# Moving four low-part subtractions at the end of attention from VectorE to GpSimd in a two-layer decoder trunk

## The chip, the cores and the metric

The kernel runs on one core of a Trainium2 chip. Its time is the device time of one execution in microseconds (us); the median of three runs of the kernel before is 1260.38 us (1257.83 to 1261.02). The engines are named as in the profile: PE is TensorE (PEld its weight loads), DVE is VectorE, ACT is ScalarE, POOL is GpSimd and SP is SyncE, which issues most DMAs.

## The reference

A trunk of two layers over 512 tokens of 1024 features, in float32. Layer 0 mixes by a causal Conformer convolution, layer 1 by differential attention with 8 heads; each is followed by a SwiGLU feed-forward network (2816 hidden) and a gate that adds a projection of a second input `p`:

```
for i in range(DEPTH):                       # DEPTH = 2
    ...                                      # i = 0: h += conformer_conv(rms_norm(h))
    lambda_init = 0.8 - 0.6 * math.exp(-0.3 * i)
    u = rms_norm(h, attn_norm_g[j])
    h = h + diff_attention(u, ...)           # i = 1
    u = rms_norm(h, ffn_norm_g[i])
    h = h + swiglu(u, ffn_w_gate[i], ffn_w_up[i], ffn_w_down[i])
    gate = jax.nn.sigmoid(rms_norm(h, ple_norm_g[i]) @ ple_w_gate[i])
    h = h + gate * (p[i] @ ple_w_proj[i])

# in diff_attention, per block of 128 queries:
    probs = jax.nn.softmax(logits, axis=-1)              # two sets of logits per head
    w = probs[:, :, 0] - lam * probs[:, :, 1]
    return jnp.einsum('bhqk,bhkd->bhqd', w, v)
```

The product `p[i] @ ple_w_proj[i]` takes 256 features of `p` to 1024. The change touches its operands in layer 1.

## The kernel before

All features lie on the 128 partitions and tokens on the free axis, so the trunk is a set of 128x512 tiles. **Precision.** Every matrix product is done as three products of rounded operands (`mm3`, lines 164 to 166): each operand is split into a high part, rounded to the type fp32r, and a low part, the rest. The high part is a cast on ScalarE; the low part is a subtraction, raw minus high. For weights this is `weight()`: a DMA from SP into a raw tile `wraw` (two buffers), the cast at line 157 into `whi`, the subtraction at line 159 into `wlo` (four buffers each). Its argument `eng` says which engine subtracts: VectorE unless told otherwise. GpSimd is told for three of the weights of the q/k projections (`GLO`). For `p`, `pfeatures` loads two 128x512 halves, casts them at line 278 and subtracts at line 279: on GpSimd in layer 0, on VectorE in layer 1. In layer 1 its raw halves use the `wraw` buffers too, so that the order there is half 0, half 1, projection weight 0, projection weight 1, and then the weights of attention's output product, each of them loaded when the subtraction two places before it is done.

**Attention.** q/k projections for pairs of heads (`unit`) and value projections (`values`) run for each block of 128 tokens; between their products, stages of the softmax of earlier heads are placed. `unit` leaves q and k with their norms: a power on GpSimd (line 229, the inverse root), then a scaling on GpSimd (line 925). `unit_end` transposes the block on PE (line 931), copies it from PSUM by ScalarE (lines 939 and 940), makes a second copy on GpSimd (944) and the low parts on VectorE (947 and 949). The stages of a head `hd` and a query block `qb` are: `stage_s`, scores on PE (976, 977), add bias and take the maximum on VectorE (979, reads PSUM), exponential on ScalarE (983), and on VectorE the weights of the difference (986 to 988); `stage_t`, transpose on PE (996), cast on ScalarE (998), low part on VectorE (999); `stage_a`, products with the values on PE (1012, 1013), gather (1019, 1020) and after the last block the head's norm (1024 to 1034, with a power at 229 and a scaling at 1034 on GpSimd); `stage_o`, transpose (1041) and split for the output product (178, 179).

**The end of attention.** After the last value projection the eight projections of `p` (`project`) run, with the remaining stages placed between by `step()`: their weights are two `weight()` tiles, one for four projections each. Then the output product begins.

**Order.** The code above is written in one sequence; a scheduler then sets each engine's order by its own estimate of durations. Each engine works through its list strictly in that order, so an instruction that waits holds all that is behind it on its engine. Changing the engine of an instruction can change the lists of all engines.

Of the kernel before, what the change touches and what calls it, by code (L numbers as in the profile page):

```python
# [15 lines left out]
ALU = mybir.AluOpType  # L16
# [76 lines left out]
def trunk(ctx, tc, xT, pT, wts, diag, dww, vec, rel, onehot, lamv, out):  # L93
    nc = tc.nc
    V, A, G, T = nc.vector, nc.scalar, nc.gpsimd, nc.tensor
# [7 lines left out]
    def sb(shape, tag, bufs, dt=F32):  # L103
        uid[0] += 1
        return pool.tile(shape, dt, tag=tag, name=f"{tag}_{uid[0]}", bufs=bufs)
# [10 lines left out]
    f = lambda ap: ap.bitcast(F32)  # L116
# [29 lines left out]
    def weight(n=1024, pieces=1, between=(), eng=V, after=None):  # L146
        i = wnext[0]
        wnext[0] += 1
        raw = sb([P, 1024], "wraw", 2)
        hi = sb([P, 1024], "whi", 4, F32R)  # L150
        lo = sb([P, 1024], "wlo", 4, F32R)
        for k in range(pieces):
            cut = slice(k * n // pieces, (k + 1) * n // pieces)
            loaded[0] = nc.sync.dma_start(raw[:, cut], wts[i, :, cut])
            if k < len(between):
                between[k]()
            A.copy(hi[:, cut], raw[:, cut])  # L157
            with tc.issue_after(after.ins) if after else nullcontext():
                eng.tensor_tensor(lo[:, cut], raw[:, cut], f(hi[:, cut]), ALU.subtract)  # L159
        return hi, lo  # L160
# [107 lines left out]
    def pfeatures(layer, parts):  # L268
        for k, (hi, lo) in enumerate(parts):
            if layer == 0:  # L270
                if k == 0:
                    two = sb([P, 2, S], "B7", 1)
                    nc.sync.dma_start(two.rearrange("p a s -> p (a s)"), pT[layer])
                raw = two[:, k]
            else:
                raw = sb([P, 1024], "wraw", 2)[:, :S]
                nc.sync.dma_start(raw, pT[layer, :, k * S : (k + 1) * S])
            A.copy(hi, raw)
            (G if layer == 0 else V).tensor_tensor(lo, raw, f(hi), ALU.subtract)
        return parts  # L280


# [2 lines left out]
    def project(ph, m, w, o, step=lambda: None):  # L285

        acc = mm()
        for k in range(2):
            last_product[0] = mm3(acc, wpart(w, 2 * (m % 4) + k), ph[k], k == 0, k == 1)
            step()  # L290
        last_copy[0] = A.copy(o, acc)
        return o
# [169 lines left out]
    for c in range(NC):  # L462
        wa, wg = pairs[c]
        if c == 0:
            pg = half(wg)
            norm.diagonal()
            pa = half(wa)
            rb = norm.rows()
            ph = pfeatures(0, [(sb([P, S], t, 2, F32R), sb([P, S], t, 2, F32R)) for t in ("wth", "wtl")])
# [590 lines left out]
    for what, at, pace in QKV:  # L1060
        ws = slab(GLO if what == "q" and at > 0 else 0, P * at[1] if what == "v" else S)
        for tb in range(4):
            if (what, at, tb) == ("v", (6, 2), 0):
                ph = pfeatures(1, [both(sb([P, 2, S], t, 1, F32R)) for t in ("B0", "B1")])
            between = take(3 * pace[tb])
            between += [None] * (6 - len(between))
            if waiting:
                between.append(partial(unit_end, *waiting))
                waiting = None
            if what == "v":  # L1070
                values(at, ws, tb, between)
            else:
                waiting = unit(at, ws, tb, between)
# [4 lines left out]
    def step():  # L1078
        if stages:
            n, s = stages.pop(0)  # L1080
            s()
        else:
            n = 99
        while done[0] < NH and (n - LA - 3) // 4 > done[0]:
            stage_o(done[0])
            done[0] += 1

    pp = []
    for m in range(NC):
        if m % 4 == 0:  # L1090
            w = weight()
        step()
        if m % 2 == 0:
            o2 = sb([P, 2, S], f"B{m // 2 + 2}", 1) if m < 4 else sb([P, 2, S], f"C{m // 2 + 1}", 2)
        pp.append(project(ph, m, w, o2[:, m % 2], step))
# [155 lines left out]
```

## Time and profile before

| | |
|---|---|
| median of 3 runs | 1260.38 us (1257.83 to 1261.02) |
| the profiled execution | 1259.05 us, of which the span from first to last instruction is 1257.3 us |
| busy in the span | PE 1239.1, DVE 904.6, ACT 615.5, POOL 264.1 us |
| granted TensorE clock, mean | 0.998 |

The times in the rows count from the start of the span. A timeline row has the start, the duration, the engine, the line, the operation, its output and inputs by the program's names with buffer numbers left out, the shape, and in brackets the idle time of the engine before it and what ended that. The sums of busy time per stretch tell which engine sets the pace there; a wait row says who ended it. Rows of one line and engine that follow each other are merged (x2).

### The profile page before, as it was taken

How to read it: one execution, taken by the hardware profiler on the slowest of the kernel's cores; microseconds unless marked ns; L12 is line 12 of the kernel's file. 1: busy time of each engine (PE TensorE's matmuls, PEld its weight loads, DVE VectorE, ACT ScalarE, POOL GpSimd, SP SyncE). 2: the span in 40 equal slices, each digit the busy share in tenths (PEclk: the TensorE clock that was granted, in tenths of full speed). 3: DMA queues.
4: the chain of work that ended last, by engine and by line, in shares of the span. 5: the costliest groups of instructions: out<-in, count | busy, mean ns of one | idle time of the engine just before them, and what ended most of it. 6: DMA issues, size and time to landing. Idle time of an engine off the chain costs nothing.

```text
span 1257.3 us, 18628 instructions
## 1 busy us (share of the span) xinstructions
PE 1239.1 (99%) x7152; PEld 1086.2 (86%) x7152; DVE 904.6 (72%) x1482; ACT 615.5 (49%) x1023; POOL 264.1 (21%) x231
## 2 busy tenths in 40 slices
PE   9999999999999999999999998999999999999998
PEld 7888778898999899988888987878898999899887
DVE  6998755965588558667678889746965598468665
ACT  6743454543355235446566768634542355235441
POOL 2853522000001000042616633122000000000030
PEclk9999999999999999999999999999999999999999
DMA  8666223464466444243322214223554467444241
GB/s 298 199 194 179 74 76 109 131 164 129 122 176 181 137 110 122 67 147 96 90 92 76 76 48 129 85 67 101 151 156 145 103 182 184 137 109 117 77 134 67
DMA packets 60597, 158.39 MB, mean 126 GB/s; under 512 B 6451, under 2 KB 11059, under 8 KB 60508
## 3 DMA queue, kind: packets, MB, share of 16 engines
q1 hardware_dynamic: 53776, 136.99, 34.3%
q0 software_dynamic: 4608, 16.78, 8.2%
q10 hardware_dynamic: 2124, 3.43, 0.9%
q8 instruction: 56, 0.92, 0.3%
q14 instruction: 33, 0.27, 0.1%
HBM read 151.91 MB, written 4.21 MB: 124 GB/s over the span
## 4 chain that ended last, share of the span: by engine, by line
PE 96%; DVE 2%; ACT 1%; DMA 0%; issue 0%; SPq 0%; ACTq 0%
PE mm L164 26%; PE mm L165 25%; PE mm L166 25%; PE tp L166 2%; PE tp L165 2%; PE tp L164 2%; PE sc L370 2%; PE sc L165 1%; PE sc L166 1%; PE sc L164 1%; PE mm L1012 1%; PE sc L976 1%; PE sc L977 1%; PE tp L996 1%; PE mm L370 1%; PE mm L326 1%
## 5 line engine op out<-in xcount | busy, mean ns | idle before, releaser
L165 PE MATMUL mm<-A,whi 128*128 128x512 f32 (+1 forms) x904 | 311.6, 346 | 0.3 <-DVE A L575 0.3
L164 PE MATMUL mm<-A,wlo 128*128 128x512 f32 (+1 forms) x904 | 307.2, 345 | 4.7 <-DVE wlo L159 3.0
L166 PE MATMUL mm<-A,whi 128*128 128x512 f32 (+1 forms) x904 | 310.0, 343 | 0.0
L157 ACT CAST whi<-wraw 128x1024 fp32r<-128x1024 f32 (+2 forms) x150 | 151.3, 1015 | 225.4 <-PE mm L166 103.8
L159 DVE TENSOR_TENSOR wlo<-wraw,whi 128x1024 fp32r<-128x1024 f32 (+2 forms) x147 | 186.3, 1270 | 61.0 <-ACT whi L157 60.3
L164 PEld LDWEIGHTS mm<-A,wlo 128*128 128x128 f32 x904 | 171.4, 190 | 26.3 <-ACT A L178 2.5
L165 PEld LDWEIGHTS mm<-A,whi 128*128 128x128 f32 x904 | 171.5, 190 | 21.8 <-issue 1.2
L166 PEld LDWEIGHTS mm<-A,whi 128*128 128x128 f32 x904 | 171.6, 190 | 20.8 <-issue 1.4
L165 PE MATMUL mm<-B,whi 128*128 128x512 f32 x368 | 143.3, 390 | 0.0
L166 PE MATMUL mm<-B,whi 128*128 128x512 f32 x368 | 143.3, 390 | 0.0
L164 PE MATMUL mm<-B,wlo 128*128 128x512 f32 x368 | 141.1, 391 | 0.0
L681 POOL DMA_DIRECT2D C<-in_wts x32 | 28.1, 878 | 512.1 <-DVE h L792 178.2
L204 POOL TENSOR_TENSOR acc<-acc,wk 128x512 f32<-128x512 f32 x35 | 56.6, 1617 | 218.3 <-ACT wk L203 110.9
L166 PEld LDWEIGHTS mm<-B,whi 128*128 128x128 f32 x368 | 69.1, 188 | 15.0
L165 PEld LDWEIGHTS mm<-B,whi 128*128 128x128 f32 x368 | 69.1, 188 | 14.3
L164 PEld LDWEIGHTS mm<-B,wlo 128*128 128x128 f32 x368 | 69.1, 188 | 14.2
L166 PE MATMUL mm<-whi,A 128*128 128x512 f32 (+1 forms) x224 | 81.1, 363 | 0.0
L164 PE MATMUL mm<-whi,A 128*128 128x512 f32 (+1 forms) x224 | 80.9, 366 | 0.0
L165 PE MATMUL mm<-wlo,A 128*128 128x512 f32 (+1 forms) x224 | 80.8, 364 | 0.0
L792 DVE TENSOR_TENSOR h<-mm,h 128x512 f32<-128x512 f32 x48 | 33.0, 688 | 64.5 <-PE mm L166 64.5
L229 POOL TENSOR_TENSOR r<-v,mhalf 128x8 f32<-128x8 f32 (+1 forms) x31 | 46.2, 1490 | 120.9 <-DVE v L227 99.9
L674 DVE TENSOR_TENSOR wlo<-wraw,whi 128x1024 fp32r<-128x1024 f32 x32 | 39.2, 1225 | 33.5 <-ACT whi L673 33.4
(271 smaller groups left out, 2674.4 us busy)
## 6 DMA issues: line engine op xcount, KB each, us to landing
wraw<-in_wts SPq DMA_DIRECT2D x162, 512.0 KB, 3.6
C<-in_wts SPq DMA_DIRECT2D x32, 512.0 KB, 4.8
C<-in_wts POOLq DMA_DIRECT2D x32, 512.0 KB, 5.8
bias<-in_wts SPq DMA_DIRECT2D x32, 256.0 KB, 3.2
wraw<-in_wts SPq DMA_DIRECT2D x16, 384.0 KB, 3.1
D<-in_diag SPq DMA_DIRECT2D x22, 256.0 KB, 4.6
C<-in_diag SPq DMA_DIRECT2D x16, 256.0 KB, 4.7
h<-in_xT SPq DMA_DIRECT2D x8, 256.0 KB, 5.4
```

Source lines behind the costliest of these rows:

```text
L157: A.copy(hi[:, cut], raw[:, cut])
L159: eng.tensor_tensor(lo[:, cut], raw[:, cut], f(hi[:, cut]), ALU.subtract)
L164: T.matmul(acc, al, bh, start=first, stop=False)
L165: T.matmul(acc, ah, bl, start=False, stop=False)
L166: return T.matmul(acc, ah, bh, start=False, stop=last)
L204: self.last = self.eng.tensor_tensor(self.acc, self.acc, sq, ALU.add)
L229: last_pow[0] = G.tensor_tensor(r[:, :n], v[:, :n], mhalf[:, :n], ALU.pow)
L326: last_tap[0] = T.matmul(acc, dg[:, j % 4], ups[c][:, j : j + S], start=(j == 0), stop=(j == PE_TAPS[c] - 1))
L370: last_tap[0] = T.matmul(acc[:, g * P : (g + 1) * P], w, ups[c][:, g, LEAD - m : LEAD - m + P], start=(m == 0), stop=(m == LAGS - 1),)
L674: V.tensor_tensor(lo, raw, f(hi), ALU.subtract)
L681: nc.gpsimd.dma_start(q, wts[i + 2].rearrange("p (a s) -> p a s", a=2), accum_op=ALU.add)
L792: V.tensor_tensor(h[m], acc, h[m], ALU.add)
```

## The change

Two edits. In `pfeatures` the low parts of `p` are subtracted on GpSimd in layer 1 as in layer 0, and the two projection weights at the end of attention are asked for with `eng=G`, so that their low parts are subtracted on GpSimd. The casts, the loads and all products stay.

```diff
@@ pfeatures @@
             A.copy(hi, raw)
-            (G if layer == 0 else V).tensor_tensor(lo, raw, f(hi), ALU.subtract)
+            G.tensor_tensor(lo, raw, f(hi), ALU.subtract)
         return parts
@@ the loop over the eight projections of p @@
     for m in range(NC):
         if m % 4 == 0:
-            w = weight()
+            w = weight(eng=G)
         step()
```

The scheduler's lists change on four engines from there to the end of attention. GpSimd's list at this place, before (`big_7390` is the last q/k block of the last pair of heads, `D_1328` a head's output, the `r` are the powers):

```order
L944 CAST C_1297_7001<-C_1297_7001 64x2x128
L229 TENSOR_TENSOR r_1361_7300<-v_1360_7298,mhalf_71 128x4
L944 CAST C_1296_7000<-C_1296_7000 64x2x128
L944 CAST C_1297_7001<-C_1297_7001 64x2x128
L1034 TENSOR_TENSOR D_1328_7133<-D_1328_7133,r_1361_7300 128x512
L229 TENSOR_TENSOR r_1383_7398<-v_1382_7396,mhalf_71 128x8
L925 TENSOR_TENSOR big_7390<-big_7390,r_1383_7398 128x512
```

and now, where `B_1390` and `B_1391` are the two low halves of `p` and `wlo_7652` and `wlo_7869` those of the two projection weights:

```order
L944 CAST C_1297_7001<-C_1297_7001 64x2x128
L279 TENSOR_TENSOR B_1390_7413<-wraw_7415,B_1390_7413 128x512
L279 TENSOR_TENSOR B_1391_7414<-wraw_7419,B_1391_7414 128x512
L229 TENSOR_TENSOR r_1361_7300<-v_1360_7298,mhalf_71 128x4
L944 CAST C_1296_7000<-C_1296_7000 64x2x128
L944 CAST C_1297_7001<-C_1297_7001 64x2x128
L1034 TENSOR_TENSOR D_1328_7133<-D_1328_7133,r_1361_7300 128x512
L229 TENSOR_TENSOR r_1383_7398<-v_1382_7396,mhalf_71 128x8
L159 TENSOR_TENSOR wlo_7652<-wraw_7650,whi_7651 128x1024
L159 TENSOR_TENSOR wlo_7869<-wraw_7867,whi_7868 128x1024
L925 TENSOR_TENSOR big_7390<-big_7390,r_1383_7398 128x512
```

The halves stand ahead of the power for `D_1328`, and the weights between the power for the last q/k block and the scaling of that block.

On PE the transpose of that block (`tp_7475`) stood ahead of the last value products of the query block that is under way (`mm_7499`). Before:

```order
L1012 MATMUL mm_7499<-B_1260_6829,wth_7459 128x256
L931 MATMUL tp_7475<-ident_65,big_7390 128x128 x4
L976 MATMUL sc_7587<-C_1192_6466,C_1190_6464 128x512
L977 MATMUL sc_7587<-C_1194_6468,C_1190_6464 128x512
L996 MATMUL tp_7527<-ident_65,big_7347 128x128
L1013 MATMUL mm_7499<-B_1260_6829,wtl_7460 128x128
L1012 MATMUL mm_7499<-B_1269_6887,wth_7459 128x256
...
L976 MATMUL sc_7703<-C_1296_7000,C_1294_6998 128x128
L977 MATMUL sc_7703<-C_1298_7002,C_1294_6998 128x128
L1012 MATMUL mm_7656<-B_1260_6829,wth_7529 128x256
L164 MATMUL mm_7696<-B_1390_7413,wlo_7652 128x512
```

Now these products come first, a score product of the next head (`sc_7740`) is taken forward, and the transpose stands behind them; `mm_7656`, which starts the next head's values, stands ahead of the projection (`mm_7696`) as before, now behind three more pairs of score products:

```order
L1012 MATMUL mm_7499<-B_1281_6971,wth_7459 128x256
L1013 MATMUL mm_7499<-B_1281_6971,wtl_7460 128x128
L976 MATMUL sc_7740<-C_1296_7000,C_1294_6998 128x256
L977 MATMUL sc_7740<-C_1298_7002,C_1294_6998 128x256
L931 MATMUL tp_7475<-ident_65,big_7390 128x128 x4
L996 MATMUL tp_7527<-ident_65,big_7347 128x128
L976 MATMUL sc_7703<-C_1297_7001,C_1295_6999 128x128
L977 MATMUL sc_7703<-C_1299_7003,C_1295_6999 128x128
L976 MATMUL sc_7740<-C_1297_7001,C_1295_6999 128x256
L977 MATMUL sc_7740<-C_1299_7003,C_1295_6999 128x256
L1012 MATMUL mm_7656<-B_1260_6829,wth_7529 128x256
L164 MATMUL mm_7696<-B_1390_7413,wlo_7652 128x512
```

On ScalarE the four copies of that block (`C_1294` to `C_1297`) stood ahead of the cast of the output product's first weight (`whi_8050`), with the cast `wth_7529`, which `mm_7656` reads, behind them. Before:

```order
L898 ACTIVATE B_1281_6971<-mm_7623,rcol_5628 128x2x128
L939 ACTIVATE C_1294_6998<-tp_7475,lam_5564 64x2x128
L940 ACTIVATE C_1296_7000<-tp_7475,vec_63 64x2x128
L939 ACTIVATE C_1295_6999<-tp_7475,lam_5564 64x2x128
L940 ACTIVATE C_1297_7001<-tp_7475,vec_63 64x2x128
L983 ACTIVATE acc_7518,st_7343<-acc_7518,st_7343 128x384
L157 CAST whi_8050<-wraw_8049 128x1024
L998 CAST wth_7529<-tp_7527 128x128
```

Now the gather and the square of a head (`D_1395`, `wk_7564`) and the cast of `whi_8050` stand ahead of the copies:

```order
L1019 COPY D_1395_7431<-mm_7499 128x256
L1024 ACTIVATE wk_7564<-D_1395_7431 128x512
L157 CAST whi_8050<-wraw_8049 128x1024
L939 ACTIVATE C_1294_6998<-tp_7475,lam_5564 64x2x128
L940 ACTIVATE C_1296_7000<-tp_7475,vec_63 64x2x128
L939 ACTIVATE C_1295_6999<-tp_7475,lam_5564 64x2x128
L940 ACTIVATE C_1297_7001<-tp_7475,vec_63 64x2x128
L998 CAST wth_7529<-tp_7527 128x128
```

The cast `wth_7529` is behind the copies in both lists.

## The prediction

> **What bounds the kernel now.** I read the page's first part, then busy time by stretches (columns: start and end, length, busy time of PE, PEld, DVE, ACT and POOL with the number of instructions, granted clock, DMA share, GB/s), then the waits of PE between 750 and 800 us (total, times, longest), then the timelines of single engines.
>
> ```profile
> PE 1239.1 (99%) x7152; PEld 1086.2 (86%) x7152; DVE 904.6 (72%) x1482; ACT 615.5 (49%) x1023; POOL 264.1 (21%) x231
> ...
> 750.00:800.00 50.00, 45.28 (x293) 39.72 (x292) 48.40 (x143) 41.75 (x103) 12.61 (x14) 0.97 0.40 122
> ...
> 800.00:830.00 30.00, 29.94 (x163) 25.37 (x161) 14.36 (x42) 10.88 (x25) 6.14 (x6) 1.00 0.09 27
> ...
> 770.00:780.00 10.00, 7.10 (x43) 5.55 (x41) 9.86 (x26) 8.34 (x21) 0.79 (x2) 1.00 0.49 146
> 780.00:790.00 10.00, 8.54 (x39) 6.48 (x40) 9.34 (x33) 7.24 (x19) 2.05 (x2) 0.83 0.45 146
> ...
> 782.00:785.00 3.00, 3.00 (x14) 2.70 (x13) 2.34 (x9) 1.44 (x4) 0.00 (x0) 0.50 0.39 149
> ```
>
> ```profile
> PE mm L1012 <- ACT wth L998: 2.0, 2, 1.1
> ...
> PE sc L976 <- DVE st L979: 1.7, 3, 0.9
> ...
> PE tp L1041 <- DVE wtl L999: 0.5, 1, 0.5
> ...
> PE tp L996 <- DVE A L179: 0.4, 1, 0.4
> ```
>
> TensorE is busy for 99% of the span, so an edit on other engines can only give back what PE loses. The edit lies between 750 and 800 us, where attention overlaps the last projections, and there PE doesn't set the pace: VectorE is busy for 48.40 of 50 us, and PE falls to 7.10 and 8.54 of 10 us. PE's waits there are 2.0 + 1.7 + 0.5 + 0.4 = 4.6 us, ended by VectorE or by a ScalarE cast. From 782 to 785 the granted clock is 0.50, so 3 us of PE time did 1.5 us of work. Relief for VectorE can bring 4.6 + 1.5 = 6.1 us at most.
>
> **What leaves VectorE.** Four subtractions, in two pairs (timeline rows: start, length in us):
>
> ```profile
> 758.70 0.96 DVE L988 SCALAR_TENSOR_TENSOR big<-rb,st,big 128x512 f32<-128x512 f32 x1
> ...
> 760.24 0.16 DVE L1030 TENSOR_TENSOR v<-v,r 128x4 f32<-128x4 f32 x1
> 760.32 1.29 DVE L279 TENSOR_TENSOR B<-wraw,B 128x512 fp32r<-128x512 f32 x2
> 761.52 0.16 DVE L227 TENSOR_SCALAR v<-v 128x4 f32<-128x4 f32 x1
> ...
> 767.06 0.34 DVE L988 SCALAR_TENSOR_TENSOR big<-acc,st,big 128x128 f32<-128x128 f32 x1
> ...
> 767.41 0.40 DVE L979 CUSTOM_DVE_ANT_0 rb<-sc,bias 128x256 f32<-128x256 f32 x1
> ...
> 767.73 2.99 DVE L159 TENSOR_TENSOR wlo<-wraw,whi 128x1024 fp32r<-128x1024 f32 x2
> 770.64 0.47 DVE L899 SCALAR_TENSOR_TENSOR B<-mm,rcol,B 128x256 fp32r<-128x256 f32 x1
> 771.03 0.54 DVE L979 CUSTOM_DVE_ANT_0 acc<-sc,bias 128x384 f32<-128x384 f32 x1
> ...
> 771.51 0.68 DVE L999 TENSOR_TENSOR wtl<-tp,wth 128x512 fp32r<-128x512 f32 x1
> ...
> 772.18 0.67 DVE L979 CUSTOM_DVE_ANT_0 big<-sc,bias 128x512 f32<-128x512 f32 x1
> ```
>
> 1.29 + 2.99 = 4.28 us off a saturated engine: the first term, -4.28.
>
> **What they cost on GpSimd.** It already forms low parts of three attention weights, and in the first layer those of p:
>
> ```profile
> L159 POOL TENSOR_TENSOR wlo<-wraw,whi 128x1024 fp32r<-128x1024 f32 x3 | 7.2, 2399 | 6.8 <-issue 6.2 <-ACT whi L157 0.6
> ...
> L159 DVE TENSOR_TENSOR wlo<-wraw,whi 128x1024 fp32r<-128x1024 f32 (+2 forms) x147 | 186.3, 1270 | 61.0 <-ACT whi L157 60.3
> ```
>
> ```profile
> 17.66 2.45 POOL L279 TENSOR_TENSOR wth<-B,wth 128x512 fp32r<-128x512 f32 x1 [16.14 <-ACT wth L278]
> ...
> 17.76 3.44 DVE L159 TENSOR_TENSOR wlo<-wraw,whi 128x1024 fp32r<-128x1024 f32 x2
> ...
> 20.08 2.26 POOL L279 TENSOR_TENSOR wtl<-B,wtl 128x512 fp32r<-128x512 f32 x1
> ```
>
> A 128x1024 subtraction takes 2.40 us. Those of 128x512 took 2.45 + 2.26 = 4.71 us for two, while VectorE's two L159 beside them took 3.44 us where two of the mean are 2.5. If a half costs half of 2.40, both engines' work end to end, 2.4 + 2.5 = 4.9 us, is about the 4.71: they took turns. So I take 1.2 us for each p half, and GpSimd gets 2 x 1.2 + 2 x 2.40 = 7.2 us of new work. It is busy for 12.61 of the 50 us; its total is no bound. What matters is the turns, and its order.
>
> **The turns.** Three more places where a wide GpSimd operation ran:
>
> ```profile
> 642.80 2.41 POOL L159 TENSOR_TENSOR wlo<-wraw,whi 128x1024 fp32r<-128x1024 f32 x1 [6.20 <-issue]
> 643.65 2.64 DVE L159 TENSOR_TENSOR wlo<-wraw,whi 128x1024 fp32r<-128x1024 f32 x1 [1.14 <-ACT whi L157]
> ...
> 672.13 2.39 POOL L159 TENSOR_TENSOR wlo<-wraw,whi 128x1024 fp32r<-128x1024 f32 x1
> 672.35 3.19 DVE L227 TENSOR_SCALAR v<-v 128x8 f32<-128x8 f32 x1
> 674.48 1.03 POOL L1034 TENSOR_TENSOR D<-D,r 128x512 f32<-128x512 f32 x1
> ...
> 708.28 2.40 POOL L159 TENSOR_TENSOR wlo<-wraw,whi 128x1024 fp32r<-128x1024 f32 x1 [0.62 <-ACT whi L157]
> 708.73 0.42 DVE L999 TENSOR_TENSOR wtl<-tp,wth 128x256 fp32r<-128x256 f32 x1
> 709.34 1.37 DVE L987 SCALAR_TENSOR_TENSOR st<-st,lam 128x1 f32<-128x1 f32 x1
> ```
>
> VectorE's subtraction at 643.65 took 2.64 us and ended 1.08 us after GpSimd's: it waited out the whole of it. At 672.35 a 128x8 operation took 3.19 us, until two GpSimd operations in a row were through. At 709.34 a 128x1 L987 ended with GpSimd's subtraction, while L999, which reads PSUM, ran in 0.42 us beside it. So what takes its tensors from SBUF (L159, L988, L987, L227, L1030) stands still while GpSimd subtracts; what reads a PSUM tensor (L979, L999, L899, L947, L949) goes on. The 2.99 us above holds such a wait too, for the L925 that runs from 767.46.
>
> The Trainium skill, page "SBUF — State Buffer", section "SBUF: two separate sides", has VectorE and GpSimd hold a shared port pair as an exclusive lock for a whole instruction, the loser blocking fully; the 2.64 us agree. By that page the four operations are paid on VectorE nearly in full and the change loses. How much depends on who goes next, where the rows differ: turns at 17.66, two in a row at 672.13.
>
> *The p halves.* L988 holds VectorE until 759.66, so the first half runs on GpSimd to 760.86. L1030, ready at 760.3, waits 0.55 us for it. Then the second half, to 762.1, holds L227: 1.2. Second term, +1.8; L227 goes at 762.15 instead of 761.52, 0.63 later. At the least nothing waits (0); without turns it is 2.4.
>
> *The weights.* GpSimd's queue now:
>
> ```profile
> 765.75 1.64 POOL L229 TENSOR_TENSOR r<-v,mhalf 128x8 f32<-128x8 f32 x1
> 767.46 1.04 POOL L925 TENSOR_TENSOR big<-big,r 128x512 f32<-128x512 f32 x1
> ```
>
> In the new order the two weights stand behind this power, L229, and ahead of L925. The power comes 0.63 later by the p halves, and 0.7 more because VectorE's L988 and L979 of 767.06 and 767.41 (0.34 + 0.40) are placed ahead of the values it needs. It ends at 765.75 + 1.3 + 1.64 = 768.7, the subtractions at 771.1 and 773.5, L925 at 774.5 instead of 768.5. These 2 x 2.40 + 1.04 = 5.84 us fall on VectorE's L979, L988, L979, L999, L899, L987, L988. With turns, the four that read PSUM (0.54 + 0.67 + 0.68 + 0.47 = 2.36) run beside it and the rest is waiting: third term, +3.5. Without turns only the first L979 runs, +5.3; at the least 0.
>
> Sum so far: -4.28 + 1.8 + 3.5 = +1.0 us.
>
> **What is late next.** L925 scales the last q/k block; PE's L931 transposes it, ScalarE copies it out in four pieces (L939, L940), and in ScalarE's order the cast L998 stands behind them, for which PE's L1012 ahead of the projection waits:
>
> ```profile
> 770.78 0.47 ACT L939 ACTIVATE C<-tp,lam 64x256 fp32r<-64x256 f32 x1 [0.54 <-PE tp L931]
> ...
> 774.55 0.39 PE L1012 MATMUL mm<-B,wth 128*128 128x256 f32 x1 [0.94 <-ACT wth L998]
> ...
> 788.58 0.40 PE L164 MATMUL mm<-B,wlo 128*128 128x512 f32 x1
> ...
> 791.12 0.39 PE L166 MATMUL mm<-B,whi 128*128 128x512 f32 x1
> ```
>
> With L925 6 us later, and ScalarE's L1019, L1024 and a weight's L157 now ahead of the copies, L1012 comes near 781 instead of 774.55. Most of that isn't lost: some score products are done ahead of it, VectorE works on meanwhile, and behind it stands a projection's pair of accumulations, as long as the one from 788.58 to 791.5 (2.9 us), in which VectorE catches up; from there it sets the pace again. What stays is where VectorE runs dry, for the last score block's exponential, for L1020, and for the first copy: three times about one ScalarE piece like the 0.47, an estimate. Fourth term, +1.4, between 0 and twice that.
>
> The next weights' raw buffers come free when GpSimd is done, some 2 us later; their products follow the last projections, so later than 791.5, and a cover of over 15 us hides it; without it 2 us would show. From 800 to 830 PE is busy for 29.94 of 30 us, so a shift made before is carried to the end.
>
> **Sum.** -4.28 + 1.8 + 3.5 + 1.4 = +2.4 us. The profiled execution took 1259.05 us, which gives 1261.5; the median of the runs, 1260.38, is 1.3 higher and gives 1262.8. I say 1262. At the low end nothing waits: -4.28, 1254.8 to 1256.1. At the high end, no turns: -4.28 + 2.4 + 5.3 + 1.4 = +4.8, and with the clock, below, +6 to +8: 1265 to 1268.
>
> **Rivals.** *The relief counts in full (faster).* VectorE is the bound, 4.28 us go, GpSimd has room, and the small operations slip in between. For it: all 4.6 us of PE's waits hang on VectorE or ScalarE. Against it: the 2.64, 3.19 and 1.37 us, and L925 behind 4.8 us of subtraction. Time: 4.28 off both bases, about 1255.5. Chance 0.12.
>
> *GpSimd's run in a row stops VectorE, and PE falls to half clock (slower).* One mechanism: from L987 to the end of L925 VectorE waits, as L227 did at 672.35; PE, without score products and with L1012 at 781 or later, idles some 5 us, and the projections behind it start at clock 0.50, as at 782. That is +4.8, and half to all of 2.9 us more for the projections: +6 to +7.7, about 1266. It decides once VectorE stands for over 4 us between 768 and 775. For it: two in a row at 672.13. Against it: the turns at 17.66, and VectorE's own operations to do. Chance 0.31.
>
> The Trainium skill, page "TensorE: Matmul & The Clock Gate", section "Part 1: The HAM clock gate (the "warmup" mystery)", puts the fall to half speed behind an idle window of about 3.4 us. Here it fell at 782 with no wait above 1.1 us before it, so waits that add up were enough; by the page only this rival's stall would do it, by the row the forecast's smaller ones could too, for up to 1.5 us more.
>
> *Forecast: within 0.3%.* Saved and paid nearly cancel. Chance 0.57.
>
> **How the numbers follow.** 0.3%, 3.8 us, is about what a measurement of this kernel tells from no change. Faster 0.12, same 0.57 and slower 0.31 are the three cases. The forecast's own range, from its third and fourth terms, is 1258 to 1265. To leave out no more than 2 in 10 it takes in most of both rivals: 1255.5 to 1267.5.
>
> **What would show it.** Right: beside GpSimd's four subtractions VectorE has L987, L988, L1030 or L227 rows lengthened by 4 to 7 us together; the last block's L925 starts near 773 to 775; the L1012 ahead of the projection runs near 780, with PE idle for several us before it; PE's busy time from 750 to 800 stays near 45 us or falls by some 2. Wrong: the small operations keep their 0.2 us, PE is over 9.5 busy from 770 to 790 and the span falls by 4; or the clock stands at 0.50 for 3 us or more at the projections and the span grows by over 4.

## The result, and the profile after

The changed kernel takes 1266.55 us (median of 6 runs, 1266.14 to 1267.97), the kernel before beside it 1259.85 us (6 runs, 1257.83 to 1261.02): 6.7 us or 0.5% slower by the medians; the ratio over all these runs is 1.0059 with a 95% interval of 1.0048 to 1.0069. The profiled execution took 1266.64 us with a span of 1264.9 us.

Busy time over the whole span, from the page of the changed kernel:

```profile
PE 1242.3 (98%) x7152; PEld 1088.4 (86%) x7152; DVE 908.5 (72%) x1478; ACT 617.1 (49%) x1023; POOL 271.8 (21%) x235
```

VectorE's total went up, from 904.6 to 908.5 us, although four operations, 4.28 us, left it. Of the 8.2 us that came in their place 5.2 are waiting that is booked as busy, shown below; the other 3 were not taken apart. GpSimd took 7.7 us more. Busy time by stretches of the changed kernel (start and end, length, busy time of PE, PEld, DVE, ACT, POOL, granted clock, DMA share, GB/s), and of the kernel before two stretches that are needed below:

```profile
750.00:800.00 50.00, 42.34 (x256) 37.03 (x254) 45.42 (x118) 36.83 (x87) 20.61 (x18) 0.86 0.36 107
800.00:830.00 30.00, 29.22 (x167) 25.11 (x168) 18.72 (x56) 15.91 (x40) 4.10 (x4) 1.00 0.17 51
830.00:850.00 20.00, 17.47 (x78) 13.97 (x77) 9.49 (x15) 7.66 (x11) 6.79 (x5) 1.00 0.21 57
```

```profile
778.47:781.88 3.41, 1.36 (x8) 0.79 (x7) 3.41 (x11) 3.02 (x8) 0.00 (x0) 1.00 0.89 246
...
830.00:850.00 20.00, 17.53 (x76) 14.19 (x77) 12.63 (x13) 10.14 (x13) 6.57 (x5) 1.00 0.39 117
```

From 750 to 800 us PE has 42.34 us in place of 45.28, VectorE 45.42 in place of 48.40, so VectorE now runs dry as well. Over the 100 us PE is idle for 100 - 42.34 - 29.22 - 17.47 = 11.0 us; before it was 100 - 45.28 - 29.94 - 17.53 = 7.2. That is 3.7 us. The clock gives the rest. The same view of the changed kernel, cut so that the edges fall where the clock changes:

```profile
767.28:770.70 3.42, 3.42 (x28) 3.33 (x27) 3.31 (x6) 1.50 (x3) 3.42 (x2) 1.00 0.01 2
770.70:774.11 3.41, 1.55 (x9) 1.06 (x8) 3.41 (x7) 1.07 (x3) 3.41 (x3) 1.00 0.50 154
774.11:777.52 3.41, 3.21 (x13) 2.92 (x14) 2.87 (x10) 1.98 (x6) 0.35 (x1) 0.50 0.50 154
777.52:780.94 3.42, 1.01 (x5) 0.61 (x3) 3.22 (x7) 2.83 (x7) 0.16 (x1) 0.50 0.25 77
780.94:784.35 3.41, 2.64 (x9) 2.35 (x10) 3.30 (x13) 2.77 (x8) 1.89 (x3) 0.50 0.53 154
784.35:787.76 3.41, 3.41 (x10) 2.64 (x9) 3.41 (x14) 1.58 (x5) 1.04 (x1) 0.50 0.24 37
787.76:791.18 3.42, 3.42 (x25) 2.94 (x23) 2.37 (x7) 2.67 (x7) 0.00 (x0) 1.00 0.30 116
```

For four stretches of 3.41 us the clock stands at 0.50. PE is busy for 3.21 + 1.01 + 2.64 + 3.41 = 10.3 us in them and does 5.1 us of work, so 5.1 us are lost; before, the one stretch at 0.50, from 781.9 to 785.3, cost 1.7. That is 3.4 us more, and 3.7 + 3.4 = 7.1 us is the growth of the span, 7.6, within half a microsecond.

Where PE's idle time hangs: its waits from 750 to 805 us (total, times, longest), and the timeline at the places that the prediction named:

```profile
PE sc L976 <- DVE st L979: 6.2, 5, 3.2
PE mm L1012 <- ACT wth L998: 0.9, 2, 0.6
```

```profile
759.26 2.86 POOL L279 TENSOR_TENSOR B<-wraw,B 128x512 fp32r<-128x512 f32 x2
760.31 0.59 DVE L1030 TENSOR_TENSOR v<-v,r 128x4 f32<-128x4 f32 x1
761.01 1.14 DVE L227 TENSOR_SCALAR v<-v 128x4 f32<-128x4 f32 x1
...
768.53 4.75 POOL L159 TENSOR_TENSOR wlo<-wraw,whi 128x1024 fp32r<-128x1024 f32 x2
768.64 2.32 DVE L987 SCALAR_TENSOR_TENSOR st<-st,lam 128x1 f32<-128x1 f32 x1
771.36 2.20 DVE L988 SCALAR_TENSOR_TENSOR big<-rb,st,big 128x256 f32<-128x256 f32 x1
...
773.22 1.24 POOL L925 TENSOR_TENSOR big<-big,r 128x512 f32<-128x512 f32 x1
777.26 1.05 PE L931 MATMUL tp<-ident,big 128*128 128x128 f32 x4
779.82 0.47 ACT L939 ACTIVATE C<-tp,lam 64x256 fp32r<-64x256 f32 x1
781.53 0.27 ACT L998 CAST wth<-tp 128x128 fp32r<-128x128 f32 x1
781.71 0.47 PE L976 MATMUL sc<-C,C 128*128 128x128 f32 x1 [3.17 <-DVE st L979]
782.73 0.41 PE L1012 MATMUL mm<-B,wth 128*128 128x256 f32 x1
782.94 0.63 PE L164 MATMUL mm<-B,wlo 128*128 128x512 f32 x1
783.37 0.63 PE L165 MATMUL mm<-B,whi 128*128 128x512 f32 x1
```

The transposes and the first projection in the kernel before:

```profile
770.14 0.60 PE L931 MATMUL tp<-ident,big 128*128 128x128 f32 x4
...
774.77 0.40 PE L164 MATMUL mm<-B,wlo 128*128 128x512 f32 x1
```

The waits for GpSimd are there: L1030 at 760.31 takes 0.59 in place of 0.16 us, L227 1.14 in place of 0.16, L987 2.32 in place of 0.21, L988 2.20 in place of 0.47. Together 0.43 + 0.98 + 2.11 + 1.73 = 5.2 us. The scaling L925 comes at 773.22 instead of 767.46, the transposes L931 at 777.26 instead of 770.14, ScalarE's copies from 779.82 instead of 770.78, and the first projection at 782.94 instead of 774.77. PE stands longest at 781.71, 3.17 us, at a score product that waits for VectorE to read the other half of its tile. Which of these is cause and which is company is what the experiments are for.

### The profile page after: what moved, and what is told of

Read it like the earlier page. It is cut to its first block, busy times and chain, and to the rows that moved or that the text cites. A ratio compares the mean times of both kernels' runs of the same rounds, so it can differ in the third digit from the quotient of the medians.

```text
span 1264.9 us, 18618 instructions
## 1 busy us (share of the span) xinstructions
PE 1242.3 (98%) x7152; PEld 1088.4 (86%) x7152; DVE 908.5 (72%) x1478; ACT 617.1 (49%) x1023; POOL 271.8 (21%) x235
## 4 chain that ended last, share of the span: by engine, by line
PE 93%; DVE 4%; ACT 1%; DMA 1%; issue 1%; SPq 0%; DVEq 0%; ACTq 0%
PE mm L164 25%; PE mm L165 25%; PE mm L166 25%; PE tp L166 2%; PE tp L165 2%; PE tp L164 2%; PE sc L370 2%; PE sc L165 1%; PE sc L166 1%; PE sc L164 1%; DMA wraw<-in_wts 1%; PE mm L1012 1%; PE mm L370 1%; PE sc L976 1%; PE tp L996 1%
## 5 line engine op out<-in xcount | busy, mean ns | idle before, releaser
L159 DVE TENSOR_TENSOR wlo<-wraw,whi 128x1024 fp32r<-128x1024 f32 (+2 forms) x145 | 183.6, 1269 | 63.9 <-ACT whi L157 63.3
```

## The experiments

All were timed in five rounds beside the kernel before. In each kernel a few lines are added, so the line numbers of its rows shift by up to 10. In the table every time of a profile is counted from the same operation, the power that stands at 754.60 us in the kernel before. PE's idle time and the loss at half clock (busy time times the missing clock) are summed over 1 us stretches of the same 100 us, as above.

| kernel | measured against before, us | first projection starts | PE idle | lost at half clock | both, against before |
|---|---|---|---|---|---|
| before | 0 | 774.8 | 7.2 | 1.7 | 0 |
| the change | +6.7 | 782.9 | 11.0 | 5.1 | +7.2 |
| p alone on GpSimd (e_p) | +1.1 | 776.3 | 7.8 | 0.0 | -1.1 |
| weights alone (e_w) | +5.2 | 780.4 | 9.9 | 4.0 | +5.1 |
| weights behind the scaling (e_scale) | +4.9 | 779.3 | 9.9 | 3.3 | +4.3 |
| relief alone (e_zero) | -2.2 | 775.1 | 6.1 | 1.5 | -1.3 |
| lock alone (e_again) | +0.9 | 773.8 | 7.6 | 3.1 | +1.8 |
| late block alone (e_pow) | +5.3 | 779.3 | 9.2 | 3.8 | +4.1 |
| the change, output weights late (e_late) | +7.1 | 783.1 | 10.3 | 4.1 | +5.5 |
| the change, PE kept busy (e_warm) | +10.5 | 786.2 | 11.8 | 4.9 | +7.9 |
| before, output weights late (c_late63) | -1.5 | 774.8 | 7.1 | 0.0 | -1.8 |
| the same, later (c_late72) | +0.9 | 774.7 | 7.7 | 1.6 | +0.4 |
| the same, apart (c_6370) | +1.1 | 775.0 | 8.3 | 1.6 | +1.1 |
| the same, a projection weight late too (c_w2) | +6.0 | 774.6 | 10.9 | 3.3 | +5.4 |

The last column agrees with the measured difference within 2.2 us for all but e_warm, which also runs eight matmuls more. Part of what is left is that the measured differences are of medians and a profile shows one execution: set beside the growth of the profiled execution from the same operation on, the last column is within 1.3 us, and within 1.8 for e_warm. The ratios given below go over all runs and put a measured difference up to 0.7 us lower or higher than the medians do. So the whole effect lies in this stretch, and it is PE's idle time and PE's clock.

### Half of the change: p alone, the weights alone

```diff
 e_p: as the change, but
-            w = weight(eng=G)
+            w = weight()
 e_w: as the change, but
-            G.tensor_tensor(lo, raw, f(hi), ALU.subtract)
+            (G if layer == 0 else V).tensor_tensor(lo, raw, f(hi), ALU.subtract)
```

> Only the two halves of p go to GpSimd; the two weights stay on VectorE. Theory A (the turns: a GpSimd subtraction stops VectorE's next operation that takes its tensors from SBUF): VectorE is rid of 1.29 us and waits 0.43 + 1.0 us at L1030 and L227, so nothing is left: within 1.5 us of the kernel before. Theory B (the queue: what hurts is L925 behind the weights): L925 at most 1.3 us late, the 1.29 us are a gain: 1 to 2 us faster. Theory C (the clock alone makes the loss): no fall beyond the present one, within 1 us.

> Only the two projection weights go to GpSimd; p stays on VectorE. Theory A: 2.99 us saved, over 4 us of waiting at L987 and L988, and what follows: 5 to 7 us slower, nearly the whole loss. Theory B: the same 5 to 7, by L925. Theory C: as much of the loss as the clock's stretch at 0.50 is long here.

With p alone: 1260.1 against 1258.97 us, ratio 1.0010 (1.0001 to 1.0019). With the weights alone: 1264.17 us, ratio 1.0036 (1.0023 to 1.0048). The timeline of p alone, then of the weights alone:

```profile
760.46 0.59 DVE L1030 TENSOR_TENSOR v<-v,r 128x4 f32<-128x4 f32 x1
761.16 1.14 DVE L227 TENSOR_SCALAR v<-v 128x4 f32<-128x4 f32 x1
```

```profile
768.38 4.75 POOL L159 TENSOR_TENSOR wlo<-wraw,whi 128x1024 fp32r<-128x1024 f32 x2
771.21 2.93 DVE L987 SCALAR_TENSOR_TENSOR st<-st,lam 128x1 f32<-128x1 f32 x2
773.09 1.04 POOL L925 TENSOR_TENSOR big<-big,r 128x512 f32<-128x512 f32 x1
```

In the first, 1.29 us leave VectorE and 1.4 us of waiting come back. In the second the scaling L925 is late and PE falls to half clock for 10.2 us. The two differences, 1.1 and 5.2, add up to 6.3 of the change's 6.7 us: nearly all of it comes with the weights.

How much p alone costs goes with the clock of the single execution. Of its eleven, the two with a mean granted clock of 1.000 take 1258.39 and 1259.19 us, the three with 0.995 take 1262.12 to 1263.17. The profile is of the first, the shortest, and has no half clock; what the median holds beyond it isn't in these rows.

### The weights behind the scaling

```diff
 e_scale: as the change, but
+        last_scale[0] = G.tensor_tensor(q3, q3, rs..., ALU.mult)     # line 925
-            w = weight(eng=G)
+            w = weight(eng=G, after=last_scale[0])
```

> As the changed kernel, but the two weights' subtractions are queued on GpSimd behind the scaling L925 of the last q/k block (line 927 here) instead of ahead of it. Theory B: L925 is back near 768 to 769, the loss goes: within 2 us of the kernel before. Theory A: the subtractions still stop VectorE for some 4 us, a little later: 4 to 7 us slower than before; at best 2 us better than the changed kernel.

Measured: 1263.91 us, ratio 1.0036 (1.0024 to 1.0049). Two microseconds come back, no more, as theory A had it. Its timeline shows why this was a weaker test than I took it for:

```profile
768.80 1.04 POOL L927 TENSOR_TENSOR big<-big,r 128x512 f32<-128x512 f32 x1
769.80 4.92 POOL L159 TENSOR_TENSOR wlo<-wraw,whi 128x1024 fp32r<-128x1024 f32 x2
...
774.61 0.61 PE L933 MATMUL tp<-ident,big 128*128 128x128 f32 x4
```

The scaling is back at 768.80, but the transposes that use it stand at 774.61, behind score products for which PE waits in its list; before they ran at 770.14. The block is late here too, by PE's order and VectorE's waits, and beside GpSimd's scaling and subtractions VectorE still stands for 3.1 us (two 128x1 operations take 1.06 and 0.67 in place of 0.21 us, one of 128x256 takes 2.23 in place of 0.47). So the run doesn't show that lateness is cheap.

### The relief alone

```diff
 e_zero: as the change, but for the four subtractions
-                    eng.tensor_tensor(lo[:, cut], raw[:, cut], f(hi[:, cut]), ALU.subtract)
+                    G.memset(f(lo[:, cut]), 0.0)
```

> As the changed kernel, but the four subtractions are left out: GpSimd fills the low parts of layer 1's p and of its two projection weights with zero, which reads nothing from SBUF. Theory A: VectorE is rid of 4.28 us and waits for nothing: 2 to 5 us faster than before, PE's waits between 750 and 800 near 1 us. Theory D (the new lists of the engines are worse in themselves, whatever GpSimd does): the lists change here too, so 2 us or more slower than before.

Measured: 1256.8 us, ratio 0.9981 (0.9972 to 0.9990). The fills depend on nothing and ran earlier, so this stretch has neither the subtractions nor a late block. VectorE's relief of 4.28 us is worth 2.2 us of time (1.3 to 3.5 by the interval), half of what leaves it. PE's waits in the 50 us that answer to 750 to 800 fell from 4.6 to 3.5 us, not to the 1 that theory A expected. The lists of its engines differ from those of both kernels, so this run doesn't clear the changed kernel's lists.

### The lock alone

```diff
 e_again: as before, and for the two projection weights
+        G.tensor_tensor(raw, raw, f(hi), ALU.subtract)
```

> As the kernel before: VectorE forms all four low parts. GpSimd repeats the subtraction of the two projection weights, in place on the raw weights that nobody reads any more, queued behind the last scaling L925. It relieves VectorE of nothing, so what it costs is the price of a wide GpSimd subtraction by itself. Theory A (VectorE stands still while GpSimd subtracts): two subtractions of 2.40 us hold VectorE's small SBUF operations for 3 to 4 us in all, seen as L227, L987, L988, L989 or L990 rows lengthened to over 1 us, and the time goes up by 3 to 6 us, to 1262 to 1265. Rival (GpSimd's work costs nothing by itself, the loss came from what is late behind it): no lengthened rows, and within 1 us of before.

Measured: 1260.67 against 1259.75 us, ratio 1.0011 (1.0002 to 1.0020). The rival's time came, within 1 us by the medians, but not its picture: VectorE does wait, though only once, and the 3 us or more of theory A didn't come:

```profile
769.82 5.67 POOL L161 TENSOR_TENSOR wraw<-wraw,whi 128x1024 f32<-128x1024 f32 x2 [1.16 <-DVE wlo L159]
773.33 2.17 DVE L989 SCALAR_TENSOR_TENSOR st<-st,lam 128x1 f32<-128x1 f32 x1
```

While GpSimd subtracts for 5.67 us, VectorE runs its own subtraction and operations that read PSUM, and one 128x1 operation stands for 2.17 us in place of 0.2. Two microseconds of waiting cost about one of time, 0.3 to 2.5 by the interval. The wait for GpSimd is real, and its price small for these 2.0 us; in the change it is 5.2 us. With the last block on time, PE's first projection starts at 773.8.

### The late block alone

GpSimd takes the last block's inverse square root four times; it reads 128x8 values, and nothing moves between the engines.

```diff
 e_pow: as before, and for the last q/k block
-        last_pow[0] = G.tensor_tensor(r[:, :n], v[:, :n], mhalf[:, :n], ALU.pow)
+        for _ in range(4):
+            last_pow[0] = G.tensor_tensor(r[:, :n], v[:, :n], mhalf[:, :n], ALU.pow)
```

> As the kernel before (VectorE forms all four low parts), but GpSimd takes the last q/k block's inverse square root four times in place of once, into the same tile: three operations of 1.64 us more, which read 128x8 values, ahead of the scaling L925. So L925 ends 4.9 us later, about as late as in the changed kernel, with nothing taken from VectorE and no wide subtraction on GpSimd. It prices the fourth term alone (predicted +1.4, between 0 and 2.8). Theory of the late block: PE waits for the late chain and falls to half clock, +2 to +5 us, 1261.5 to 1264.5. Rival (a late L925 is hidden, as VectorE has enough to do; what costs in the changed kernel is VectorE standing still): within 1 us of before. No VectorE row beside the three operations is lengthened to over 1 us.

Measured: 1264.18 against 1258.92 us, ratio 1.0037 (1.0024 to 1.0051): +5.3 us by the medians, 4.7 by the ratio, 3.0 to 6.4 by its interval. Its timeline, and PE's busy time with the edges where the clock changes:

```profile
767.62 7.55 POOL L230 TENSOR_TENSOR r<-v,mhalf 128x8 f32<-128x8 f32 x4
769.60 2.36 DVE L159 TENSOR_TENSOR wlo<-wraw,whi 128x1024 fp32r<-128x1024 f32 x2
775.24 1.04 POOL L926 TENSOR_TENSOR big<-big,r 128x512 f32<-128x512 f32 x1
776.34 1.11 PE L932 MATMUL tp<-ident,big 128*128 128x128 f32 x4 [1.62 <-POOL big L926]
779.42 0.58 PE L977 MATMUL sc<-C,C 128*128 128x256 f32 x1 [1.75 <-DVE st L980]
780.80 0.58 PE L1013 MATMUL mm<-B,wth 128*128 128x256 f32 x1 [0.59 <-ACT wth L999]
781.18 0.63 PE L164 MATMUL mm<-B,wlo 128*128 128x512 f32 x1
```

```profile
772.69:776.10 3.41, 1.84 (x11) 1.40 (x11) 2.68 (x10) 2.48 (x6) 3.25 (x3) 1.00 0.72 259
776.10:779.51 3.41, 1.42 (x6) 1.02 (x6) 3.41 (x8) 2.44 (x5) 0.18 (x1) 0.50 0.32 76
779.51:782.93 3.42, 2.83 (x8) 2.15 (x9) 3.36 (x9) 2.88 (x10) 1.12 (x2) 0.50 0.68 184
782.93:786.34 3.41, 3.41 (x10) 2.64 (x9) 2.19 (x9) 0.59 (x1) 1.00 (x1) 0.50 0.31 127
```

VectorE's two subtractions take 2.36 us beside the powers, so the powers hold nothing up; a later one, at 775.41, takes 1.96 in place of 1.22 us beside the scaling. PE waits 1.62 us for the scaling itself, 1.75 for a score reading, 0.59 for the cast ahead of the projection, then does the projections at half clock: (1.42 + 2.83 + 3.41) / 2 = 3.8 us lost. One late operation, without any subtraction moved, costs most of what the change costs. The scheduler knew of it and set its lists accordingly, much as in the change (in the traces PE's order here and in the change differ in 23 rows, those of before and of the change in 70); so this is the price of a late block with the lists that come with it, and how it divides between the two stays open.

### Taking the longest wait away

I took PE's wait of 3.17 us at 781.71 for a cause of its own: VectorE's list has the first output weight's subtraction ahead of the score reading for which PE waits.

```diff
 e_late: as the change, but
+        mixed[hd, qb] = V.scalar_tensor_tensor(es[0][:, :n], ...)     # line 988
-    linear(NC, ot, add_attn, 2, heads_until, step)
+    linear(NC, ot, add_attn, 2, heads_until, step, first=(mixed[6, 3], mixed[6, 3], None))
```

> As the changed kernel (all four subtractions on GpSimd), but the low parts of the first two output weights, which VectorE forms, are queued behind the score mixing of head 6's last block. In the changed kernel the first of them stands in VectorE's list at 779.95 us, ahead of the score reading L979 of 781.37 for which PE waits 3.17 us, and itself waits for ScalarE's cast of 778.88 us. Ring theory (the fourth term was mis-sized because work that is late is queued in VectorE's list ahead of the score reading): the 3.17 us wait goes, PE's idle time from 750 to 850 falls by 3 us or more, and the time comes to 1261 to 1264. Rival (the waits for GpSimd's lock and the late last block are all of it): PE then waits for the late block's cast L998 in its place, and the time stays within 1 us of 1266.5.

Measured: 1266.38 against 1259.30 us, ratio 1.0059 (1.0042 to 1.0075), the same as the change. This theory falls. The wait shrank by 1.28 us, and nothing came of it, since the late block stands where it stood (this profile runs 1.2 us behind that of the change throughout):

```profile
781.67 0.47 PE L977 MATMUL sc<-C,C 128*128 128x128 f32 x1 [1.89 <-DVE st L980]
...
782.76 0.27 ACT L999 CAST wth<-tp 128x128 fp32r<-128x128 f32 x1
```

### Keeping PE busy

```diff
 e_warm: as the change, but ahead of the first projection's products
+            with tc.issue_after(warm.ins):            # the last block's transposes
+                for _ in range(8):
+                    T.matmul(acc, ones_r, ph[0][0], start=True, stop=True)
```

> As the changed kernel, with 8 matmuls more: they fill the first projection's tile before its real products overwrite it, and stand on TensorE behind the last q/k block's transposes, so in the stretch in which PE waited (about 777 to 782). Theory C (half clock): the projections ran at clock 0.50 from 782.9 to 788.1, 5.1 us in place of 2.8, because PE had idled; if that is a loss of its own, the busy PE keeps its clock, the projections take near 3 us, and about 2.3 us of the 7 come back: near 1264. Rival: the ring of waits between VectorE, ScalarE and PE sets the end, the half clock only fills time in which PE would wait anyway; then the time stays at 1266 or goes up by the extra matmuls' time (8 at 0.2 to 0.4 us, some 2 us) where they are in the way.

Measured: 1270.25 against 1259.75 us, ratio 1.0084 (1.0070 to 1.0097). The scheduler put the eight matmuls behind the wait instead of into it:

```profile
784.53 3.54 PE L291 MATMUL mm<-B,ones 128*128 128x512 f32 x8
787.91 0.40 PE L164 MATMUL mm<-B,wlo 128*128 128x512 f32 x1
...
790.43 0.39 PE L166 MATMUL mm<-B,whi 128*128 128x512 f32 x1
```

They ran at half clock for 3.54 us; the twelve products behind them start 0.23 us apart, where in the change they start 0.43 apart. A busy PE gets its clock back, but whether the half clock costs time of its own, or only fills time in which PE would wait, isn't settled by this run.

### The output weights' low parts later on VectorE

The same queueing as in e_late, but on the kernel before: c_late63 behind head 6's last block, c_late72 behind head 7's third, c_6370 one behind each of head 6's last and head 7's first, c_w2 as c_late63 with the second projection weight behind head 6's second block as well.

```diff
 c_late63: as before, but
-    linear(NC, ot, add_attn, 2, heads_until, step)
+    linear(NC, ot, add_attn, 2, heads_until, step, first=(mixed[6, 3], mixed[6, 3], None))
 c_w2: as c_late63, and
-            w = weight()
+            w = weight(after=mixed[6, 1] if m else None)
```

> As the kernel before, all subtractions on VectorE, but the low parts of the first two output weights (2.4 us of VectorE, needed only when the output products begin, after 800) are queued behind the score mixing of head 6's last block, so behind the stretch in which VectorE sets the pace. Theory A (between 750 and 800 VectorE is the bound and PE loses 4.6 us of waits and 1.5 us at half clock; what leaves VectorE there without a lock is worth about what it was worth when the four subtractions were left out): 2.4 of 4.28 us leave, so 1 to 2 us faster, 1257 to 1258. Rival: the waits hang on the chain of one block and not on VectorE's sum, then within 0.5 us; or the output products now wait for the weights, then slower by up to 2.4 us.

> As the run with the two output weights queued late, but behind the mixing of head 7's third block, later still. Theory A: the same 1 to 2 us faster, if the output products begin after them; rival: they are formed too late and the output products wait, seen as PE waiting for VectorE's L159 after 800, and up to 3 us slower.

> As the kernel before, with the first output weight's low part queued behind the mixing of head 6's last block and the second's behind that of head 7's first block, so that they don't stand in one piece of 2.35 us ahead of the score readings. If that piece still cost PE a wait near 795: 0.5 us faster than the run in which both stood behind head 6's last block, 1257.5 to 1258.5; if the pace there is VectorE's sum, the same as that run.

> As the run in which both output weights are queued behind the mixing of head 6's last block, and the second projection weight's low part (1.2 us of VectorE, formed near 769, needed only by the third pair of projections at 792) is queued behind the mixing of head 6's second block. If what leaves VectorE between 768 and 786 is worth its time: 1 us faster than that run, 1257 to 1258, with PE's idle time from 770 to 780 below 2 us. Rival: the wait only moves to 786 to 792, the same 1258.2, or the third pair waits for it, up to 1 us slower.

Measured: c_late63 1258.23 against 1259.75 us, ratio 0.9992 (0.9983 to 1.0000); c_late72 1260.67, ratio 1.0010 (1.0001 to 1.0019); c_6370 1260.35 against 1259.30, ratio 1.0004 (0.9996 to 1.0013); c_w2 1265.31, ratio 1.0049 (1.0036 to 1.0061). The first is at the edge of what can be told from the kernel before. It beats the changed kernel clearly; in its profiled execution PE idles as long as before, 7.1 us, and what it gains is that the clock never falls:

```profile
780.00:790.00 10.00, 8.64 (x49) 6.55 (x50) 9.50 (x34) 8.26 (x21) 2.04 (x2) 1.00 0.23 81
```

Its two neighbours don't bear the gain out. c_6370 should have been half a microsecond faster than c_late63 or the same, and is 2.1 us slower. c_late72 is 0.9 us slower than before, but not by its rival's sign: PE waits 1.7 us for an output weight's low part after 800, and does so in the kernel before as well.

c_w2 was a clear miss. Nothing is on GpSimd in it that wasn't before, the first projection starts on time, and yet it loses 6.0 us, by other waits of the same stretch:

```profile
PE mm L1013 <- ACT wth L999: 5.0, 3, 2.0
PE tp L1042 <- DVE A L179: 2.2, 1, 2.2
```

Queueing one 1.2 us subtraction 14 us later made the scheduler set the lists of VectorE and ScalarE anew. Which of these moves makes the casts L999 late wasn't followed further.

## Why the prediction was right or wrong

**What bounds the kernel: right.** The effect lies where it was looked for, between 750 and 805 us, and from 805 on the shift is carried to the end.

**First term, -4.28, "off a saturated engine": too large.** The relief alone, with lists of its own, measured -2.2 us. The saturation was read from VectorE's 48.40 of 50 us. A likely reason, which no run takes apart, is that in a chain that goes round VectorE, ScalarE and PE an operation less on one engine partly becomes a wait for another. The ceiling of 6.1 us from PE's waits and clock wasn't come near.

**Second and third term, +1.8 and +3.5: right in VectorE's time.** Measured 1.4 and 3.8 us of waiting, with turns, in the operations named (L1030, L227, L987, L988). The Trainium skill, page "SBUF — State Buffer", section "SBUF: two separate sides", with its lock for a whole instruction, agrees: 2.32 and 2.20 us are waits for one subtraction of 2.4 us each. But a microsecond that VectorE waits isn't one of time either: 2.0 us in e_again cost 0.9 (0.3 to 2.5), and p alone, -1.29 + 1.4 on VectorE, cost 1.1 (0.1 to 2.4).

**Fourth term, "What is late next", +1.4 between 0 and twice that: the step that failed.** Alone, with the lists that come with it, it measures +5.3 us (3.0 to 6.4). The chain was named rightly: L925 late, the transposes late, the copies late, the cast L998 behind them, L1012 ahead of the projection. L1012 was put near 781 us and came at 782.73. What was wrong is the sentence that "most of that isn't lost", since "VectorE works on meanwhile, and behind it stands a projection's pair of accumulations [...] in which VectorE catches up". VectorE had not enough to do without PE's next scores: from 750 to 800 it is busy for 45.42 us in the change, 5.2 of them standing, against 48.40. The projection is no cover, because PE does it at half clock: from 782.94 on its products start 0.43 us apart, so that its twelve take 5.2 us, where twelve at the 0.23 us of full clock take 2.8. The term had no part for the clock, which the prediction kept for its slower rival, although the kernel before shows half clock at 782 behind waits of at most 1.1 us. The other thing that could be late, the next weights, was covered as it said: PE's one wait for a weight's low part between 800 and 870 us is 1.75 us at 842.45, and 1.75 us at 835.49 in the kernel before.

**The sum.** With the terms as measured: the relief -2.2, the late block +5.3, and 5.2 us of waiting at the 0.9 per 2.0 us of e_again, +2.3, give +5.4, where the change measured +6.7; by the ratios in place of the medians it is -2.4 + 4.7 + 3.6 = +5.9 of +7.4. The 0.9 per 2.0 is rough, by its interval. Single runs of parts need not add up exactly; the sign and most of the size are there.

**The forecast and the rivals.** The likeliest case, within 0.3%, didn't come, and the forecast's own range, 1258 to 1265, was missed; 1266.55 lies in the wide range only because that was drawn around the rivals as well. The slower rival came with its number, about 1266, and with its picture: PE out of score products, projections at clock 0.50. Its point of decision was wrong. It was to decide "once VectorE stands for over 4 us between 768 and 775"; VectorE stood for 3.8 us and took its turns, as the forecast had it, and the half clock came all the same. What costs most by e_pow is the lateness of the last block with the lists that come with it, which the forecast had in its sum and priced too low. Of the marks that were to show the forecast right, the lengthened rows and L925 at 773 came; PE's busy time from 750 to 800 fell by 2.9 us and not "some 2"; and the mark for its being wrong, clock 0.50 at the projections and a span longer by over 4 us, came too. The faster rival fails twice: the waits are there, and even without them its 4.28 us would have been 2.2.

## What to carry to other kernels

Before an operation is given to an in-order engine with room, look at what stands behind it in that engine's list: here 4.8 us of subtraction ahead of one 1.04 us scaling cost more than the saved work could bring. A share of 97% busy doesn't make every microsecond taken from that engine a microsecond of time; leave the work out in one run and see what it is worth. And where TensorE waits anyway, count the clock with the waits: the account of idle time plus loss at half clock explained nearly every run here to about 2 us.

## What the runs showed of the hardware

**The clock moves in steps of 3.41 us.** In 12 of the 14 profiles the granted clock fell to 0.50 in this stretch, each time for once, twice, three or four times 3.41 us (3.42 before, 13.65 in the change, 10.24 in e_pow, 6.83 in e_again). Cut at those edges, every step at full clock in which PE was busy for at most 54% was followed by half clock, none with more than 66% was, and those between went either way. In the change it is the step from 770.70 with 1.55 of 3.41 us, 45%; before, that from 778.47 to 781.88 with 40%. From half clock it came back after steps with 96% or more and stayed after those with 94% or less; at 95% both were seen. In the change 94%, 29% and 77% kept it at 0.50, and only the fourth, with 100%, ended it. The Trainium skill, page "TensorE: Matmul & The Clock Gate", section "Part 1: The HAM clock gate (the "warmup" mystery)", has a free-running window of 3413 ns, and the lengths agree. It gives an idle window as the cause of the fall, and for one kernel frequent short idle times between groups of matmuls, without saying how much is enough. Here only one such step, in e_w, was nearly idle, with 7%, and elsewhere a third to three fifths of a window of waits was enough.

**What the lock spares.** Powers on GpSimd over 128x8 values, 7.55 us of them in a row, left VectorE's subtractions at 2.36 us for two; they themselves took 1.89 us each in place of 1.64, and one of them, at 754.60 in the kernel before, took 2.47 beside such a subtraction. What made VectorE wait here were above all GpSimd's wide subtractions and its scalings, small operations of VectorE too: beside the scaling L1034 at 786.25 in the change, an L987 takes 1.00 in place of 0.21 us.
